# A product that needs no activations, moved to the head of a one-layer encoder step and carried through DRAM; the third FFN pair's splits moved ahead of the second pair's convolution

## The chip, the cores and the metric

The kernel runs on one core of one Trainium2 chip. The metric is the device time of one execution in microseconds: 2164.75 us before, the median of three runs (2163.62, 2164.75 and 2166.86). The profile is of one further execution, which took 2162.19 us.

## The reference, cut to what matters

One trunk layer over 1024 prompt frames and 64 sample frames (T = 1088 columns in the kernel), D_MODEL = 1024, D_FF = 2816, PLE_DIM = 256, all in fp32:

```
h = rms_norm(x, norm_mix)
glu_a, glu_b, q, k, v, gates = split(h @ w_in)
c = silu(layer_norm(dwconv31(glu_a * sigmoid(glu_b)))) @ w_conv_out
a = band_attention(q, k, v) @ w_att_out
x = x + (sigmoid(gate_c) * c + sigmoid(gate_a) * a) @ w_out
h = rms_norm(x, norm_ffn)
up, gate = split(h @ w_ffn_up)
x = x + (gelu(dwconv3(up)) * gate) @ w_ffn_down
h = rms_norm(x, norm_ple)
x = x + sigmoid(h @ w_ple_gate) * (p @ w_ple_proj)
y = rms_norm(x, norm_final)
```

`p` is an input, so `p @ w_ple_proj` (256 by 1024) depends on nothing that the layer computes.

## The kernel before

Everything lies feature-major: a tile holds 128 features (partitions) by T columns, and the columns go in three groups `GR` of 384, 384 and 320. An fp32 product is made of three passes over values split into a high and a low part (high by high, high by low, low by high): the lines L159 to L161 in the helper `mm3`, L817 to L819 in the head, L1171 to L1173 in the FFN. So a 1024-deep product for 128 output features and one group is 24 matmuls. Weights come raw from DRAM on SP's DMA queue (`w_load`); ACT makes the high part (L134, L797), DVE the low part (L135, L800). The program is written under a manual schedule: each engine runs its instructions in the order in which the code issues them, and waits only where an operand or a buffer is not ready.

**Head.** Fourteen warm-up matmuls (L743) keep TensorE busy while x arrives. The squares of the first group of x are taken by ACT (L754) and added by DVE (L761), TensorE sums them over the partitions (L770), POOL takes the power (L782), and TensorE spreads the result over the partitions (L216, `hr_ps`); twelve more warm-ups (`W2`) stand around that. Then a loop over slots `sl` follows, whose contents are set by tables (`SQ`, `ADD`, `COL`, `TOT`, `SPR`, `LAG`, `HDVE`): in a slot DVE makes one normalized tile `hn` (L187), ACT its high part `hT` (L189), DVE or POOL its low part (L181), and TensorE multiplies the tiles of earlier slots with the first two weight units (`gb` and `ga`). Behind the three groups, the ordinary jobs over the other units of `w_in` begin, `q` first.

**FFN.** The up projection works in pairs of units i = 0..21. Pairs 0 and 1 are plain. From pair 2 on a pair is computed as seven products of half size (A11·B11, S2·T2, A12·B21, S1·T1, S3·T3, S4·B22, A22·T4, in this order, 24 matmuls of 272 columns in each half, so 24 per product), whose operands are sums of activations (`comb`, T1 to T4) and of weights (`prep_a`, `prep_b`, `prep_c`; high parts by ACT L1148, sums by DVE L1157, low parts by DVE L1065). A result takes two of six PSUM banks, and is emptied by ACT (`put`, L1247) or by DVE into a sum (`add`, L1254). The convolution of a pair, `conv_a`, is one ACT pass (L1272), two DVE taps (L1275) and a gelu on ACT (L1277). Before the change, `conv_a(1)` stands ahead of pair 2, and `comb("T1")` and `prep_b(2)` behind pair 2's first `put`.

**Tail.** The down projection runs in four chunks of units. In the last one a generator `ple_prep` loads p and `w_ple_proj` (POOL's queue) and splits them. Then `ple(f, g)` makes for each feature tile f and group g the 24 matmuls with `w_ple_gate` and the 6 of p with `w_ple_proj` (L159 to L161, `pj<-pP,wpp`), a tanh on ACT (L1574), and two DVE operations (L1575, which reads the p product in PSUM, and L1578). The square and its sum for the final norm follow (L1017, L1018). Two further strands of work hang in a queue with due times and are forced where a stage needs them: `norm_ple` of the next group (hn L187, high part L189, low part L181 on POOL) and the split of the next weight unit (`wbig`, L134 and L135). The statistics of a group go through L202 (TensorE), L203, L206 (the power on POOL) and L216 (`sp_ps`).

In the changed kernel the line numbers are higher: by 1 in the helpers (L187 is L188, L135 is L136), by 66 in the head (L761 is L827), by 95 in the FFN (L1148 is L1243, L1254 is L1349), by 74 in the last stage (L1575 is L1649).

Of the kernel before, what the change touches and what calls it, by code (L numbers as in the profile page):

```python
# [16 lines left out]
P = 128  # L17
# [58 lines left out]
def encoder_step(ctx: ExitStack, tc: tile.TileContext, I, O):  # L76
# [143 lines left out]
    with tc.manual_schedule():  # L220
# [40 lines left out]
        for g, (c0, n) in enumerate(GR):  # L261
            for f in range(KT):
                dma_in(out=xt[f][:, c0:c0 + n], in_=I["x"][:, f, c0:c0 + n])
            if g == 0:
                w_load()
                dma_in(out=ident, in_=I["ident"])
                dma_in(out=par, in_=I["par"])
                w_load()
# [13 lines left out]
        hsq = [at.tile([P, KW], F32, tag=f"K{h}", name="hsq") for h in range(2)]  # L282
        hd = {}
# [512 lines left out]
        def w_hi(u, a, b):  # L796
            nc.scalar.activation(out=w2[u][:, 0, a:b, :], in_=raws[u][:, a:b, :], func=AF.Copy)  # L797
# [43 lines left out]
        for f in range(KT):  # L841
            head_acc(0, f)
            head_add(0, f)
        w_hi(0, 0, KT)
# [12 lines left out]
        ws["split"] = ws["used"] = 2  # L857
        for sl in range(3 * KT + 3 + LAG[2]):
            g, k = divmod(sl, KT)
            if g < 3:  # L860
                if k == 0:
                    begin(g)
                next(parts[g])
                pre(sl)
                if k == KT - 1:
                    next(parts[g])
            if 0 <= sl - 1 < 3 * KT:
                prod("gb", *divmod(sl - 1, KT))
# [483 lines left out]
        def prep_b(i):  # L1352
            wq[i, "A22"] = w_one()
            w_high(i, "A22")
            w_low(i, "A22")
            wq[i, "S1"], wq[i, "S3"] = w_two()
            w_high(i, "S1")
            w_sum(i, "S3")
            w_high(i, "S3")
            wq[i, "A12"] = w_one()  # L1360
            w_high(i, "A12")
            w_low(i, "S1")
            w_low(i, "S3")
            w_low(i, "A12")
# [84 lines left out]
        pP, wpp, h3, rows = [], [], [], []  # L1449

        def ple_prep():

            praw = bp.tile([P, 2, T], F32, tag="pb", name="praw")
            dma_st(out=praw, in_=I["p"])
            wraw = bp.tile([P, KT, 2, P], F32, tag="pb", name="wraw")
            dma_st(out=wraw, in_=I["w_ple_proj"])
            yield
            for k in range(2):
                t = bp.tile([P, 2, T], F32R, tag="pb", name="pP")
                split_into(t, 0, T, praw[:, k, :])  # L1460
                pP.append(t)
                yield
            wpp.extend(bp.tile([P, KT, 2, P], F32R, tag="pb", name="wpp") for _ in range(2))
            nc.scalar.activation(out=wpp[0], in_=wraw, func=AF.Copy)
            nc.vector.tensor_tensor(out=wpp[1], in0=wraw, in1=wpp[0].bitcast(F32), op=ALU.subtract)
            yield
# [16 lines left out]
        ple_it = ple_prep()  # L1483
        for ci, ch in enumerate(chunks[:-1]):
# [23 lines left out]
            for f in range(f0, KT):  # L1508
# [15 lines left out]
                if ci == 2:  # L1524
                    if f < 2:
                        next(ple_it)
                    if f in ROWS:
                        rows.append(w_use())
# [37 lines left out]
        def ple(f, g, hl):  # L1566
# [96 lines left out]
```

## Time and profile before

| | before |
|---|---|
| median of three runs | 2164.75 us |
| the profiled execution | 2162.19 us |
| its span, first to last instruction | 2160.1 us |
| TensorE (PE) busy | 2120.9 us, 98% of the span |
| VectorE (DVE) busy | 1361.8 us, 63% |
| ScalarE (ACT) busy | 829.3 us, 38% |
| GpSimd (POOL) busy | 229.1 us, 11% |
| mean granted TensorE clock | 0.995 of full speed |
| moved by DMA | 192.54 MB, 93 GB/s over the span |

The span is what the profile's times count from; the execution's own time is 2.1 us longer. Times in rows are microseconds from the start of the span. A row of a timeline gives the start, the duration (for several instructions that follow each other: from the first's start to the last's end), engine, line, operation, output and inputs, sizes and count, and in brackets how long the engine had been idle and what it waited for. A matmul's duration includes its way through the array: matmuls overlap, so what one costs is the distance of two starts.

### The profile page before, as it was taken

Reading aid. Unit: us, or ns where it says so; the run is one execution under the profiler, and the core shown is the slowest. Engines: PE = TensorE matmul, PEld = TensorE weight load, DVE = VectorE, ACT = ScalarE, POOL = GpSimd, SP = SyncE. Lnnn points to the kernel's source line nnn. Section 1 sums busy time; section 2 is a strip of 40 time slices with the busy share of each in tenths; the row PEclk is TensorE's granted clock in tenths of the full one; section 3 lists DMA queues with packets and bytes.
Section 4 is the critical chain, followed back from the end, with each engine's and each line's share of the span. In section 5 each row is a group of like instructions: output and inputs, shape, how many; then the busy total and the mean of one; then the engine's idle time right before and its main releaser. Section 6 shows DMA issues by size and latency. Waiting matters only on the chain.

```text
span 2160.1 us, 35720 instructions
## 1 busy us (share of the span) xinstructions
PE 2120.9 (98%) x14544; PEld 2088.8 (97%) x14544; DVE 1361.8 (63%) x2310; ACT 829.3 (38%) x1695; POOL 229.1 (11%) x455
## 2 busy tenths in 40 slices
PE   8999999999999999999999998999999999999997
PEld 6999999999999999999999998999999999999997
DVE  6877777777776756443254557777777763345644
ACT  5443535444444446562022334333333331113421
POOL 5110101101010101110000000000000020000400
PEclk9999999999999999999999999999999999999999
DMA  3312121212121222125433341122121253331011
GB/s 135 110 38 93 62 89 48 95 52 88 51 88 52 93 75 70 65 74 193 170 129 110 118 141 51 67 84 84 67 90 61 80 203 128 125 117 46 11 59 54
DMA packets 64708, 192.54 MB, mean 89 GB/s; under 512 B 8368, under 2 KB 22976, under 8 KB 63200
## 3 DMA queue, kind: packets, MB, share of 16 engines
q1 hardware_dynamic: 43072, 104.00, 14.2%
q0 software_dynamic: 21328, 85.71, 11.1%
q8 instruction: 114, 1.87, 0.3%
q10 hardware_dynamic: 144, 0.56, 0.1%
q14 instruction: 50, 0.41, 0.1%
HBM read 146.18 MB, written 54.01 MB: 93 GB/s over the span
## 4 chain that ended last, share of the span: by engine, by line
PE 84%; issue 7%; DVE 4%; ACT 2%; DMA 1%; POOL 1%; POOLq 0%; SPq 0%; DVEq 0%; ACTq 0%
PE pj L159 14%; PE pj L161 13%; PE pj L160 13%; PE pj L1173 7%; PE pj L1171 7%; PE pj L1172 7%; PE o_ps L520 5%; PE pj L1474 3%; PE pj L1473 3%; PE pj L1472 3%; PE t_ps L504 3%; PE s_ps L481 2%; PE s_ps L483 2%; DVE acc L1018 1%; DMA out_k_new<-kst 1%
## 5 line engine op out<-in xcount | busy, mean ns | idle before, releaser
L159 PE MATMUL pj<-hT,whl 128*128 128x384 f32 (+1 forms) x1296 | 442.0, 341 | 3.7 <-ACT kst L705 1.8
L161 PE MATMUL pj<-hT,whl 128*128 128x384 f32 (+1 forms) x1296 | 424.8, 328 | 0.3 <-DVE whl L135 0.3
L160 PE MATMUL pj<-hT,whl 128*128 128x384 f32 (+1 forms) x1296 | 424.1, 327 | 0.0
L327 DVE SCALAR_TENSOR_TENSOR c<-u,cc,c 128x1118 f32<-128x1118 f32 x240 | 331.0, 1379 | 3.2
L159 PEld LDWEIGHTS pj<-hT,whl 128*128 128x128 f32 x1296 | 244.1, 188 | 8.3 <-ACT kst L705 2.8
L161 PEld LDWEIGHTS pj<-hT,whl 128*128 128x128 f32 x1296 | 243.5, 188 | 0.6 <-DVE whl L135 0.6
L160 PEld LDWEIGHTS pj<-hT,whl 128*128 128x128 f32 x1296 | 244.1, 188 | 0.0
L1171 PE MATMUL pj<-mp,wq 128*128 128x272 f32 x704 | 203.9, 290 | 5.9 <-ACT wq L1148 5.9
L1173 PE MATMUL pj<-mp,wq 128*128 128x272 f32 x704 | 204.2, 290 | 0.0
L1172 PE MATMUL pj<-mp,wq 128*128 128x272 f32 x704 | 203.7, 289 | 0.0
L134 ACT ACTIVATE whl<-raw 128x1024 fp32r<-128x1024 f32 (+3 forms) x100 | 100.2, 1002 | 220.4 <-PE pj L1474 132.8
L135 DVE TENSOR_TENSOR whl<-raw,whl 128x1024 fp32r<-128x1024 f32 (+3 forms) x100 | 115.7, 1158 | 86.3 <-ACT whl L134 86.0
L1148 ACT ACTIVATE wq<-raw 128x512 fp32r<-128x512 f32 x144 | 84.4, 625 | 189.8 <-DVE raw L1157 124.0
L487 DVE CUSTOM_DVE_ANT_0 s<-s_ps,bias 128x640 f32<-128x640 f32 (+3 forms) x144 | 95.2, 661 | 90.3 <-PE s_ps L483 82.1
L1474 PE MATMUL pj<-gp,whl 128*128 128x384 f32 (+1 forms) x432 | 141.2, 327 | 0.6 <-DVE whl L135 0.6
L1473 PE MATMUL pj<-gp,whl 128*128 128x384 f32 (+1 forms) x432 | 141.2, 327 | 0.3 <-DVE gp L1382 0.3
L1472 PE MATMUL pj<-gp,whl 128*128 128x384 f32 (+1 forms) x432 | 141.0, 326 | 0.0
L1171 PEld LDWEIGHTS pj<-mp,wq 128*128 128x128 f32 x704 | 133.8, 190 | 6.1 <-ACT wq L1148 6.1
L520 PEld LDWEIGHTS o_ps<-v,pt 128*128 128x128 f32 (+2 forms) x1120 | 133.5, 183 | 6.4 <-issue 4.0
L1172 PE MATMUL pj<-bq,wq 128*128 128x272 f32 x480 | 138.4, 288 | 0.0
L1173 PE MATMUL pj<-bq,wq 128*128 128x272 f32 x480 | 138.2, 288 | 0.0
L1171 PE MATMUL pj<-bq,wq 128*128 128x272 f32 x480 | 138.0, 287 | 0.0
(260 smaller groups left out, 4901.3 us busy)
## 6 DMA issues: line engine op xcount, KB each, us to landing
raw<-in_w_in SPq DMA_DIRECT2D x56, 512.0 KB, 3.2
raw<-in_w_ffn_up SPq DMA_DIRECT2D x44, 512.0 KB, 4.4
q_d<-ug POOLq DMA_DIRECT2D x22, 544.0 KB, 3.0
gp<-q_d POOLq DMA_DIRECT2D x22, 544.0 KB, 7.1
tg<-s_d POOLq DMA_DIRECT2D x16, 544.0 KB, 3.9
aP<-a_d POOLq DMA_DIRECT2D x8, 1088.0 KB, 6.0
a_d<-aT POOLq DMA_DIRECT2D x64, 128.0 KB, 2.2
f_d<-e_d POOLq DMA_DIRECT2D x16, 383.5 KB, 4.9
```

The lines of the kernel that those rows point to most:

```text
L135: nc.vector.tensor_tensor(out=hl[:, 1, 0:k, :], in0=raw[:, 0:k, :], in1=hl[:, 0, 0:k, :].bitcast(F32), op=ALU.subtract)
L159: nc.tensor.matmul(ps, lhsT=wsel(hl, 0, k), rhs=r[:, 0, c0:c0 + n], start=(k == 0), stop=False)
L160: nc.tensor.matmul(ps, lhsT=wsel(hl, 0, k), rhs=r[:, 1, c0:c0 + n], start=False, stop=False)
L161: nc.tensor.matmul(ps, lhsT=wsel(hl, 1, k), rhs=r[:, 0, c0:c0 + n], start=False, stop=(k == K - 1))
L327: nc.vector.scalar_tensor_tensor(out=c_t[f], in0=u_t[f][:, j:j + CCOL], scalar=pc("conv_dw", f * CW + j), in1=c_t[f], op0=ALU.mult, op1=AL ...
L520: nc.tensor.matmul(o_ps[0:m, 0:64], lhsT=pt[0:w, b * P:b * P + m], rhs=c["v"][0:w, st["vb"] + b, h * 64:h * 64 + 64], start=(b == 0), stop ...
L1171: nc.tensor.matmul(ps, lhsT=q[:, 0, kt, :], rhs=h, start=start and kt == 0, stop=False)
L1172: nc.tensor.matmul(ps, lhsT=q[:, 0, kt, :], rhs=l, start=False, stop=False)
L1173: nc.tensor.matmul(ps, lhsT=q[:, 1, kt, :], rhs=h, start=False, stop=stop and kt == 3)
L1472: nc.tensor.matmul(ps, lhsT=hl[:, 0, k, :], rhs=h, start=k == 0, stop=False)
L1473: nc.tensor.matmul(ps, lhsT=hl[:, 0, k, :], rhs=l, start=False, stop=False)
L1474: nc.tensor.matmul(ps, lhsT=hl[:, 1, k, :], rhs=h, start=False, stop=k == K - 1)
```

## The change

1. **The product of p at the head.** p is loaded by groups and `w_ple_proj` by feature tiles, on SP's queue: 20 loads (`p_load`, `wp_load`), of which 6 of p and 2 of the weight stand ahead of the first group of x, 2 in the middle of it, 2 behind it; tiles 6 and 7 come behind all of x. ACT and DVE split them (`p_split` L320 and L322, `wp_split` L327 and L328). `p_proj(f)` makes 6 matmuls for each group (L339 to L341), 144 in all. A result is copied out of PSUM (L346 on ACT where 3f+g is even, L344 on DVE where it is odd) into the upper half of the raw p buffer, at the columns of its group: one staging place per group, so that the copy of tile f+1 waits until the store of tile f has read it. The store to DRAM (`p_d`, L347) goes by POOL's queue, 24 stores. Tiles 0 to 5 stand ahead of the first slot, tiles 6 and 7 in slots 1 to 6 (`PSL`). The squares of x's first group stand behind the passes 0, 1 and 2, as two, two and four; the statistics stand behind pass 3, the spread behind pass 4, the split of the first two weight units between. The twelve warm-ups `W2` go.
2. **FFN.** `comb("T1")` and `prep_b(2)` move ahead of `conv_a(1)`, and `prep_b` splits A12 first in every pair.
3. **Tail.** `ple_prep` goes, with its two loads and its splits. Eight loads of 544 KB bring `p_d` back into SBUF (`p2t`) at the start of the last chunk. `ple(f, g)` has no product of p any more; its first DVE operation reads `p2t`.

```diff
+PSL = {1: (6, 0, "t"), 2: (6, 1, "t"), 3: (6, 2, "s"), 4: (7, 0, "s"), 5: (7, 1, "t"), 6: (7, 2, "s")}
-W2 = (6, 6)
...
+        p_load(0)
+        wp_load(0)
+        wp_load(1)
+        p_load(1)
+        p_load(2)
+        x_load(0, range(0, 4))
+        wp_load(2)
+        wp_load(3)
+        x_load(0, range(4, 8))
+        dma_in(out=ident, in_=I["ident"])
+        wp_load(4)
+        wp_load(5)
+        w_load()
+        dma_in(out=par, in_=I["par"])
+        w_load()
+        x_load(1, range(KT))
+        x_load(2, range(KT))
...
+        def p_proj(f, gs=range(3), ps_of=None):
+            w = wpr[f % 4]
+            for g in gs:
+                c0, n = GR[g]
+                ps = ps_of if ps_of is not None else pjp.tile([P, 512], F32, tag="pj", name="pj")
+                for k in range(2):
+                    h, l = [x[:, c0:c0 + n] for x in ppt[k]]
+                    nc.tensor.matmul(ps[:, 0:n], lhsT=w[:, 0, k, :], rhs=h, start=k == 0, stop=False)
+                    nc.tensor.matmul(ps[:, 0:n], lhsT=w[:, 0, k, :], rhs=l, start=False, stop=False)
+                    nc.tensor.matmul(ps[:, 0:n], lhsT=w[:, 1, k, :], rhs=h, start=False, stop=k == 1)
+                sg = praw[1][:, c0:c0 + n]
+                if (3 * f + g) % 2:
+                    nc.vector.tensor_copy(sg, ps[:, 0:n])
+                else:
+                    nc.scalar.activation(out=sg, in_=ps[:, 0:n], func=AF.Copy)
+                dma_st(out=p_d[f][:, c0:c0 + n], in_=sg)
...
+        p_split(0)
+        wp_split(0)
+        p_split(1)
+        p_split(2)
+        wp_split(1)
+        p_proj(0)
...
+        acc0((0, 1))
+        p_proj(1)
+        wp_split(2)
+        acc0((2, 3))
+        p_proj(2)
+        wp_split(3)
+        acc0((4, 5, 6, 7))
+        p_proj(3)
         head_col(0, 0)
         head_tot(0, 0)
         head_col(0, 1)
         head_tot(0, 1)
+        wp_split(4)
+        p_proj(4)
+        w_hi(0, 0, KT)
+        head_spread(0)
         w_lo(0, 0, KT, nc.vector)
+        wp_split(5)
         w_hi(1, 0, KT)
         w_lo(1, 0, 4, nc.gpsimd)
         w_lo(1, 4, KT, nc.gpsimd)
-        warm(W2[0])
-        head_spread(0)
-        warm(W2[1])
+        p_proj(5)
...
         def prep_b(i):
+            wq[i, "A12"] = w_one()
+            w_high(i, "A12")
+            w_low(i, "A12")
             wq[i, "A22"] = w_one()
...
         plain(1, 2, 1)
+        comb("T1")
+        prep_b(2)
         conv_a(1)
         for i in range(2, NF):
             last = i == NF - 1
             put(i, "g0", both(banks(), i, "A11", "B11"))
             if i == 2:
-                comb("T1")
-                prep_b(2)
                 up_load(3, (0,))
...
+        for j in range(4):
+            t = bp.tile([P, 2, T], F32, tag="pb", name="p2t")
+            for k in range(2):
+                dma_st(out=t[:, k, :], in_=p_d[2 * j + k])
+            p2t.append(t)
...
-            p2 = pjt()
-            mmg(p2[:, 0:n], None, pP, c0, n, K=2, wsel=lambda _, s, k, f=f: wpp[s][:, f, k, :])
             z = tmp384()
             nc.scalar.activation(out=z[:, 0:n], in_=ps[:, 0:n], func=AF.Tanh, scale=0.5)
-            nc.vector.scalar_tensor_tensor(out=z[:, 0:n], in0=z[:, 0:n], scalar=1.0, in1=p2[:, 0:n], op0=ALU.add,
+            nc.vector.scalar_tensor_tensor(out=z[:, 0:n], in0=z[:, 0:n], scalar=1.0, in1=p2t[f // 2][:, f % 2, c0:c0 + n], op0=ALU.add,
                                            op1=ALU.mult)
```

DVE in the head, before: the sums of the squares, the statistics, the low part of the first weight unit, then the first normalized tiles.

```order
L761 TENSOR_TENSOR hsq<-hsq 128x384 x6
L777 TENSOR_SCALAR cc<-st_ps 128x3
L779 TENSOR_TENSOR cc<-cc,st_ps 128x3
L800 TENSOR_TENSOR whl<-raw,whl 128x1024
L187 SCALAR_TENSOR_TENSOR hn<-xt,cc,hr_ps 128x384 x3
L181 TENSOR_TENSOR hT<-hn,hT 128x384
L187 SCALAR_TENSOR_TENSOR hn<-xt,cc,hr_ps 128x384
```

DVE at the same place now (`wpr` is a split tile of `w_ple_proj`, `praw` the staging place, `pj` and `p_ps` the PSUM banks of the p product):

```order
L866 TENSOR_TENSOR whl<-raw,whl 128x1024
L328 TENSOR_TENSOR wpr<-wraw,wpr 128x256
L344 COPY praw<-pj 128x384
L344 COPY praw<-pj 128x320
L188 SCALAR_TENSOR_TENSOR hn<-xt,cc,hr_ps 128x384
L328 TENSOR_TENSOR wpr<-wraw,wpr 128x256
L188 SCALAR_TENSOR_TENSOR hn<-xt,cc,hr_ps 128x384 x2
L182 TENSOR_TENSOR hT<-hn,hT 128x384
L328 TENSOR_TENSOR wpr<-wraw,wpr 128x256
L344 COPY praw<-p_ps 128x384
L188 SCALAR_TENSOR_TENSOR hn<-xt,cc,hr_ps 128x384
```

Two copies of pass 5 stand in front of the first `hn`, and between the `hn` of the first group stand the splits of the tiles 6 and 7 and a copy of pass 6.

ACT at the second pair of the FFN, before: the convolution's two passes (L1272, L1277) stand ahead of T1 (`mp`) and of the weight splits.

```order
L1272 ACTIVATE ct<-ug,cc 128x1090
L1277 ACTIVATE ct<-ct 128x1090
L1247 ACTIVATE ug<-pj 128x272 x2
L1058 ACTIVATE mp<-x 128x544 x4
L1148 ACTIVATE wq_13030<-raw 128x512
L1148 ACTIVATE wq_13033<-raw 128x512 x2
```

ACT at the same place now:

```order
L1153 ACTIVATE mp<-x 128x544 x4
L1243 ACTIVATE wq_13247<-raw 128x512
L1243 ACTIVATE wq_13250<-raw 128x512
L1243 ACTIVATE wq_13253<-raw 128x512 x2
L1367 ACTIVATE ct<-ug,cc 128x1090
L1372 ACTIVATE ct<-ct 128x1090
L1342 ACTIVATE ug<-pj 128x272 x2
```

T1 and four weight splits stand ahead of both passes of the convolution, and the emptying of A11·B11 (L1342, `put`) behind them.

DVE in the tail, at the end of the first features' first two groups, before: `hn` of the last tile of the third group (128x320) stands ahead of the second feature's second group (L1575, 128x384).

```order
L135 TENSOR_TENSOR wbig<-raw,wbig 128x1024
L187 SCALAR_TENSOR_TENSOR tmp_19487<-x,cc,sp_ps 128x320
L1575 SCALAR_TENSOR_TENSOR tmp_19487<-tmp_19487,pj 128x384
L1578 SCALAR_TENSOR_TENSOR x<-tmp_19487,x 128x384
L1018 TENSOR_TENSOR acc_19486<-acc_19486,tmp_19487 128x384
L135 TENSOR_TENSOR wbig<-raw,wbig 128x1024
L1575 SCALAR_TENSOR_TENSOR tmp_19487<-tmp_19487,pj 128x320
```

DVE at the same place now:

```order
L188 SCALAR_TENSOR_TENSOR tmp_19732<-x,cc,sp_ps 128x320 x3
L1649 SCALAR_TENSOR_TENSOR tmp_19732<-tmp_19732,p2t 128x384
L1652 SCALAR_TENSOR_TENSOR x<-tmp_19732,x 128x384
L1113 TENSOR_TENSOR acc_19731<-acc_19731,tmp_19732 128x384
L136 TENSOR_TENSOR wbig<-raw,wbig 128x1024
L188 SCALAR_TENSOR_TENSOR tmp_19732<-x,cc,sp_ps 128x320
L1649 SCALAR_TENSOR_TENSOR tmp_19732<-tmp_19732,p2t 128x320
```

The last `hn` of the third group now stands behind that feature's three operations and behind a weight split, directly ahead of the third group's own first result.

## Rows read from the trace of the kernel before

**Rows 1.** The page: TensorE's share, and the chain of waits that ended last, by engine.

```profile
PE 2120.9 (98%) x14544; PEld 2088.8 (97%) x14544; DVE 1361.8 (63%) x2310; ACT 829.3 (38%) x1695; POOL 229.1 (11%) x455
...
PE 84%; issue 7%; DVE 4%; ACT 2%; DMA 1%; POOL 1%; POOLq 0%; SPq 0%; DVEq 0%; ACTq 0%
```

**Rows 2.** Busy time by stretch, head (columns: stretch, length, engines, clock, DMA share, GB/s).

```profile
7.14:17.18 10.04, 7.91 (x31) 5.00 (x31) 5.45 (x11) 6.18 (x12) 4.67 (x4) 0.66 1.04 373
17.18:28.35 11.17, 9.82 (x58) 8.40 (x56) 9.07 (x19) 5.23 (x13) 8.53 (x9) 1.00 0.44 160
28.35:51.30 22.95, 21.34 (x127) 19.03 (x126) 16.62 (x32) 12.28 (x28) 13.01 (x16) 1.00 0.01 1
```

**Rows 3.** Timeline of PE, head: the first product, the first job.

```profile
17.18 0.52 PE L817 MATMUL pj<-hT,whl 128*128 128x384 f32 x1
...
51.30 0.37 PE L159 MATMUL pj<-hT,whl 128*128 128x384 f32 x1
```

**Rows 4.** Timeline of DVE, head.

```profile
6.41 3.05 DVE L761 TENSOR_TENSOR hsq<-hsq 128x384 f32<-128x384 f32 x6 [5.20 <-ACT hsq L754]
...
15.43 1.66 DVE L187 SCALAR_TENSOR_TENSOR hn<-xt,cc,hr_ps 128x384 f32<-128x384 f32 x3 [2.56 <-PE hr_ps L216]
...
25.74 0.16 DVE L777 TENSOR_SCALAR cc<-st_ps 128x3 f32<-128x3 f32 x1 [1.19 <-PE st_ps L770]
...
27.15 0.60 DVE L187 SCALAR_TENSOR_TENSOR hn<-xt,cc,hr_ps 128x384 f32<-128x384 f32 x1
```

**Rows 5.** DMA issues: KB each, median us to landing.

```profile
s_d<-sg POOLq DMA_DIRECT2D x30, 192.0 KB, 2.2
...
xt<-in_x SPq DMA_DIRECT2D x16, 192.0 KB, 4.3
```

**Rows 6.** Groups by line and form, ACT: a copy of 384 columns out of PSUM.

```profile
L715 ACT ACTIVATE vst<-pj 128x384 f32<-128x384 f32 x16 | 7.9, 491 | 34.9 <-DMA out_k_new<-kst 23.0 <-PE pj L161 11.9
```

**Rows 7.** Timeline of PE, tail: blocks of six matmuls of p, and what follows each.

```profile
2039.66 0.33 PE L159 MATMUL pj<-pP,wpp 128*128 128x384 f32 x1
...
2040.70 0.33 PE L159 MATMUL pj<-gp,whl 128*128 128x384 f32 x1
...
2049.41 0.31 PE L159 MATMUL pj<-pP,wpp 128*128 128x320 f32 x1
...
2050.29 0.31 PE L159 MATMUL pj<-gp,whl 128*128 128x320 f32 x1
```

**Rows 8.** Timeline of PE, FFN pair 2: A12·B21, first of S1·T1, S4·B22.

```profile
1335.65 0.60 PE L1171 MATMUL pj<-mp,wq 128*128 128x272 f32 x1 [5.87 <-ACT wq L1148]
...
1341.38 0.29 PE L1173 MATMUL pj<-mp,wq 128*128 128x272 f32 x1
...
1347.51 0.29 PE L1171 MATMUL pj<-mp,wq 128*128 128x272 f32 x1
```

**Rows 9.** Busy time by stretch, FFN pair 2 (columns as in rows 2).

```profile
1335.00:1340.00 5.00, 4.35 (x17) 4.04 (x18) 4.15 (x9) 2.23 (x5) 0.77 (x3) 0.50 0.45 160
```

**Rows 10.** Timeline of ACT, FFN pair 2.

```profile
1324.10 1.29 ACT L1272 ACTIVATE ct<-ug,cc 128x1090 f32<-128x1090 f32 x1
1328.20 1.12 ACT L1277 ACTIVATE ct<-ct 128x1090 f32<-128x1090 f32 x1 [2.81 <-DVE ct L1275]
...
1329.77 2.29 ACT L1058 ACTIVATE mp<-x 128x544 fp32r<-128x544 f32 x4
```

**Rows 11.** Timeline of DVE, tail: last `hn` of the third group, and what stood behind it.

```profile
2046.42 0.54 DVE L187 SCALAR_TENSOR_TENSOR tmp<-x,cc,sp_ps 128x320 f32<-128x320 f32 x1
2047.88 0.55 DVE L1575 SCALAR_TENSOR_TENSOR tmp<-tmp,pj 128x384 f32<-128x384 f32 x1 [0.91 <-ACT tmp L1574]
...
2050.63 1.22 DVE L135 TENSOR_TENSOR wbig<-raw,wbig 128x1024 fp32r<-128x1024 f32 x1 [0.39 <-ACT wbig L134]
```

**Rows 12.** Timeline of POOL, tail: the power, and the last low part of the third group.

```profile
2031.88 1.16 POOL L206 TENSOR_TENSOR cc<-cc 128x3 f32<-128x3 f32 x1
...
2047.54 0.88 POOL L181 TENSOR_TENSOR h<-tmp,h 128x320 fp32r<-128x320 f32 x1 [4.29 <-ACT h L189]
```

More of the change, by code (lines that the diff above doesn't have):

```diff
@@ L260, in encoder_step @@
         xt = [xc.tile([P, CCOL], F32, tag="xc", name="xt") for _ in range(KT)]
[L261 to L268, printed above, removed]
+        p_d = dram.tile([KT, P, T], F32, name="p_d")
         nc.vector.memset(ones, 1.0 / D)
@@ L282, in encoder_step @@
         hsq = [at.tile([P, KW], F32, tag=f"K{h}", name="hsq") for h in range(2)]
+        praw = [xc.tile([P, UW], F32, tag="u", name="praw", bufs=2) for _ in range(2)]
+        ppt = [[at.tile([P, UW if tg == "lnb" else T], F32R, tag=tg, name="pp") for tg in tgs]
+               for tgs in (("Q0", "Q1"), ("vst", "lnb"))]
+        wraw = at.tile([P, 6, 2, P], F32, tag="v", name="wraw")
+        wpr = [at.tile([P, 2, 2, P], F32R, tag="pt", name="wpr", bufs=2) for _ in range(2)]
+        wpr += [at.tile([P, 2, 2, P], F32R, tag=f"bias{h}", name="wpr") for h in range(2)]
@@ new lines, in p_load, with wp_load, x_load @@
+        def p_load(g):
+            c0, n = GR[g]
+            for k in range(2):
+                dma_in(out=praw[k][:, c0:c0 + n], in_=I["p"][:, k, c0:c0 + n])
+        def wp_load(f):
+            dma_in(out=wraw[:, f % 6], in_=I["w_ple_proj"][:, f])
+        def x_load(g, fs):
+            c0, n = GR[g]
+            for f in fs:
+                dma_in(out=xt[f][:, c0:c0 + n], in_=I["x"][:, f, c0:c0 + n])
+        p_load(0)
[3 more added lines that the diff above has]
+        p_load(2)
@@ new lines, in encoder_step, with p_split @@
+        x_load(0, range(0, 4))
[10 more added lines that the diff above has]
+        x_load(2, range(KT))
+        def p_split(g):
+            c0, n = GR[g]
+            for k in range(2):
+                nc.scalar.activation(out=ppt[k][0][:, c0:c0 + n], in_=praw[k][:, c0:c0 + n], func=AF.Copy)
+            for k in range(2):
+                nc.vector.tensor_tensor(out=ppt[k][1][:, c0:c0 + n], in0=praw[k][:, c0:c0 + n],
+                                        in1=ppt[k][0][:, c0:c0 + n].bitcast(F32), op=ALU.subtract)
@@ L840, in encoder_step, with acc0 @@
         warm(WARM)
[L841 to L844, printed above, removed]
+        p_split(0)
[4 more added lines that the diff above has]
+        p_proj(0)
+        def acc0(fs):
+            for f in fs:
+                head_acc(0, f)
+                head_add(0, f)
+        acc0((0, 1))
[6 more added lines that the diff above has]
+        p_proj(3)
         head_col(0, 0)
@@ L872, in encoder_step @@
             post(sl)
+            if sl in (0, 2):
+                wp_split(6 + sl // 2)
+            if sl in PSL:
+                f, g, x = PSL[sl]
+                if x not in p_ps:
+                    p_ps[x] = (ps_t if x == "t" else ps_s).tile([P, 2, 512], F32, tag=x, name="p_ps")
+                    p_ps[x + "n"] = 0
+                p_proj(f, (g,), p_ps[x][:, p_ps[x + "n"] % 2, :])
+                p_ps[x + "n"] += 1
             for x in range(3):
@@ L1448, in encoder_step @@
             dma_st(out=xr[f], in_=x_d[f])
[L1449 to L1466, printed above, removed]
+        h3, rows, p2t = [], [], []
         def down(ps, hl, gs, g, ks, K):
@@ L1523, in encoder_step @@
                     g_split(nxt[0][0])
[L1524 to L1528, printed above, removed]
+                if ci == 2 and f in ROWS:
+                    rows.append(w_use())
         new_acc(384)
@@ L1534, in encoder_step @@
         h3.extend(gs)
+        h3.extend([bp.tile([P, 2, T], F32R, tag="pb", name="h3") for _ in range(KT - nk)])
+        for j in range(4):
+            t = bp.tile([P, 2, T], F32, tag="pb", name="p2t")
+            for k in range(2):
+                dma_st(out=t[:, k, :], in_=p_d[2 * j + k])
+            p2t.append(t)
         for g, (c0, n) in enumerate(GR):
```

17 lines of the change are left out of this document (9 added, 8 removed).

## The prediction

> **What bounds the kernel now.** The page's shares come first: TensorE is busy for 98% of the span and makes 84% of the chain that ended last [rows 1]. So a matmul that goes is worth its cadence, work for other engines is free where TensorE keeps running, and the change decides itself in the few places where it does not. The table by stretch shows the largest: between 7.14 us and the first job at 51.30, TensorE works at two thirds of its clock until the first product at 17.18, and is then busy 9.82 of 11.17 and 21.34 of 22.95 us [rows 2, 3]; warm-up matmuls are in the first figure. Next I read the head's timeline of DVE, since what starts a product there is the normalized tile `hn`: its first starts at 15.43 behind the squares' sums, its last of the first group at 27.15 [rows 4]. The third view is TensorE's timeline at FFN pair 2, with a wait of 5.87 us [rows 8], and the fourth the tail, where the six matmuls per tile and group that go can be seen between the others [rows 7].
>
> **Tail: what is removed.** A block of six took 2040.70 − 2039.66 = 1.04 us with 384 columns and 2050.29 − 2049.41 = 0.88 with 320 [rows 7]. There are 16 of the one and 8 of the other: 16.6 + 7.0 = −23.6 us. Not all of it stays. The units of feature 0 and 1 run while the norms of the next groups are made by DVE, ACT and POOL at their own pace, and the removed blocks were cover for that. Before, the last `hn` of the third group starts at 2046.42, and its low part on POOL ends 2.0 us later, at 2048.42 [rows 11, 12], ahead of its use. Now the order puts this `hn` behind feature 1's middle group: behind its two DVE operations, the sum of the square and a weight split. From the first of these to the split's end passed 2050.63 + 1.22 − 2047.88 = 4.0 us [rows 11]; with some 0.8 for the tanh ahead and the 2.0 behind, the low part is ready 6.8 us behind the middle group's last product, and TensorE wants it after 21 products and one, 22 × 0.146 = 3.2: a pause of 3.6. By the same working the low parts of the second group come 1.4 us late in feature 0, and the spread, which loses the block between it and the statistics, waits 1.15 for the power of 1.16 [rows 12]. About 0.9 us of pauses that stood there before fall into these. 1.4 + 1.15 + 3.6 − 0.9 = +5.2, and the last tanh, which ran beside the last block, adds 0.4. **Tail: −23.6 + 5.6 = −18.0.** The eight loads of `p2t` lie beside the last chunk's some 50 us of products and cost nothing; without that cover, their 4.5 MB at 373 GB/s [rows 2] would cost 12.
>
> **Head, up to the first norm.** What is added: 144 matmuls at the cadences 1.04/6 = 0.174 and 0.88/6 = 0.146 [rows 7], a pass of three groups 12 × 0.174 + 6 × 0.146 = 2.96 us; 8 passes 23.7. But a pass can't follow another at that pace, for a group has one staging place: a copy out of PSUM (0.49 [rows 6]), the store until it lands, then the next copy. No row shows a store from this place beside the head's loads. The nearest below is a store of the same size on the same queue in a quiet stretch, 2.2 us; the nearest above, the head's own loads of that size in full traffic, 4.3 [rows 5]. I take 3.2, between them, since the queue is the former's and the traffic the latter's. A turn is 0.49 + 3.2 + 0.1 = 3.8. The passes 0 to 2 end at 10.2, 13.5 and 17.5 (the first right behind p's splits and the warm-ups' end at 7.14). ACT and DVE run in order, so the last four squares stand behind the copies of pass 2, which wait for the stores of pass 1: squares at 18.7 to 20.7, sums at 21.2, against 9.46 before (6.41 + 3.05 [rows 4]). Pass 3 ends at 22.6; statistics 24.0; pass 4 27.0; spread 28.0; pass 5 waits for its weight split, which stands behind that of the first `w_in` unit, and runs from 29.0 to 32.65. DVE's two copies of pass 5 stand in front of `hn`: first `hn` at 33.2 against 15.43, **+17.8**. With 2.2 us for the landing it would be 1 us less, with 4.3 2.3 more.
>
> The Trainium skill (DMA: Bandwidth & Descriptors, § SWDGE vs HWDGE vs iDMA) says that DMAs of GpSimd and of SP feed different queues inside each DMA engine, which takes turns between them. By it a store would not wait behind the loads that are queued, and its landing would lie near the quiet row; the sum would come out some 1 us lower.
>
> **Head, the first group's slots.** From the first to the last `hn` before: 27.15 − 15.43 = 11.7 us. DVE gets in between: two splits of `w_ple_proj` and copies of passes 6 and 7. Own work 0.37 × 2 + 0.5 × 3 = 2.2; waits for ACT, which makes the high parts behind queued squares, 1.5 and 2.3; waits for the copies' matmuls, which TensorE reaches only behind the products of that slot, 2.0 and 2.2. Less about 1 us of the wait for the statistics that stood there (1.19 [rows 4]): **+9.1**. An idle 0.6 ahead of the next group's `hn` goes. Beyond, TensorE is full [rows 2] and nothing changes. **Head: +26.3**, the first job at 77.6 instead of 51.30. POOL issues 24 stores more, some of them ahead of the power and of the low parts; it is idle for more than half of that time [rows 2]. The tiles 6 and 7 of the weight land near 33 us by 373 GB/s [rows 2], 2 us before they are used.
>
> **FFN.** Before, A12·B21 waits 5.87 us for its split and then runs at half clock: 1335.65 to 1341.4, 5.75 us for 24 matmuls which take 3.0 at the cadence 0.125, at a granted clock of 0.50 in that stretch [rows 8, 9]. The lost time is 5.87 + 2.75 = 8.6 and S4·B22 starts at 1347.51. Now ACT makes T1 (2.29) where the convolution began, at 1324.10 [rows 10], A12 is split by 1327, and A12·B21 follows S2·T2 without a wait, 1329.6 to 1332.6. But ACT's two convolution passes and the gelu's wait for DVE (1.29, 2.81, 1.12 [rows 10]) now stand ahead of the copies that empty A11·B11's banks, at 1335.0. With six banks, two each for A11·B11, S2·T2 and A12·B21, S1·T1 has none and waits 2.9 us; S3·T3 waits 0.45 for the sum that empties S2·T2's banks, S4·B22 3.5 for the next sum, which stands on DVE behind T4 and more splits. S4·B22 starts at 1345.4: **−2.1**. The pause moves more than it goes. In later pairs A12 first costs nothing, since splits there are done a product ahead.
>
> **Sum.** 26.3 − 2.1 − 18.0 = +6.2: the profiled execution goes from 2162.19 to 2168.4, and the median, which stands 2.56 above it, to **2171.0**. A measurement of this kernel can tell about 0.2%, 4.3 us, from no change.
>
> **Rivals.**
> *A, faster: the copies in the head never hold ACT or DVE.* Then TensorE's time sets the head: it has at most the 10.04 us ahead of the first product and the 1.35 + 1.61 of gaps behind it [rows 2] to spare, 13.0 for the 23.7 of p, so the head grows by 10.7: 10.7 − 2.1 − 18.0 = −9.4, 2155.4. It comes out faster by over 4.3 us where the head grows by less than 2.1 + 18.0 − 4.3 = 15.8, so that, with 9.1 − 0.6 for the slots, the first `hn` starts before about 22.7. For it: the stores may land at 2.2 us. Against: ACT's and DVE's fixed order, in which the squares stand behind copies. 0.15.
> *B, no change: the third group's norm is not late.* The tail then keeps 23.6 − 0.4 = 23.2, and the sum is +1.0: 2165.8. For it: POOL and ACT are nearly idle in the tail; against: `hn` stands behind a split in the order. 0.22.
> *C, slower: the clock falls in the new pauses.* In the head, TensorE has gaps from pass 1 on, and the warm-ups that filled such gaps are gone; before, it had 0.66 of its clock in 10 us with twelve of them [rows 2]. At half clock a pass takes 5.9 instead of 2.96 and no longer hides beside the staging turn of 3.8: 2.1 more for each of three to five passes; in the FFN the price is 2.75 a product [rows 8]. 2173.8 with the FFN's alone, 2180 with three passes of the head's. The Trainium skill (TensorE: Matmul & The Clock Gate, § Why this matters for your kernels) asks for no gaps between products for this reason. 0.10.
> *The forecast* has the rest, 0.53; by the ends of the store's landing (−1.0, +2.3) and the errors of the waits, 0.04 of it falls within 0.2%.
>
> **How the numbers follow.** Faster 0.15 (A). Same 0.22 + 0.04 = 0.26. Slower 0.49 + 0.10 = 0.59. The range leaves out most of A and the far end of C: it runs from **2159 to 2182**. The likeliest case's own range is 2167 to 2176.
>
> **What would show it.** First `hn` of the head near 33, its last of the first group near 54, first job near 77.6. DVE's and ACT's waits in the head named after the landing of `p_d`. In the FFN three pauses of about 2.9, 0.45 and 3.5 us, released by ACT's `put` and DVE's `add`, and none ahead of A12·B21. In the tail a pause of about 3.6 us ahead of the last of feature 0's third-group products, released by POOL's low part. Wrong would be: a first `hn` before 22.7 (A), no pause in the tail (B), a granted clock near 0.5 in the head's passes or behind the FFN's pause (C).

## The result and the profile after

The changed kernel takes 2198.19 us (median of 4 runs, 2195.3 to 2200.5) against 2165.01 (median of 4, 2163.62 to 2166.86): slower by a factor of 1.0157, 95% interval 1.0144 to 1.017. The forecast was 2171.0 with a range to 2182; the side was right, and the time lies 16 us above the range. The profiled execution's span is 2194.3 us against 2160.1, +34.2.

Where the 34.2 us lie is read by marks, instructions that both kernels have, at their start in both TensorE timelines:

| mark on TensorE | before | after | later by | forecast |
|---|---|---|---|---|
| first job of the unit `q` | 51.30 | 90.91 | 39.6 | 26.3 |
| A11·B11 of pair 2 | 1323.61 | 1361.00 | 37.4 | 26.3 |
| S4·B22 of pair 2 | 1347.51 | 1383.04 | 35.5 | 24.2 |
| last chunk's second matmul | 1968.87 | 2013.71 | 44.8 | 24.2 |
| first matmul of the third group, feature 0 | 2045.90 | 2088.50 | 42.6 | |
| the same, feature 1 | 2050.29 | 2100.71 | 50.4 | |
| end of the span | 2160.1 | 2194.3 | 34.2 | 6.2 |

The page of the changed kernel, TensorE's share and the chain by engine, answers to [rows 1]:

```profile
PE 2132.5 (97%) x14532; PEld 2098.6 (96%) x14532; DVE 1370.1 (62%) x2333; ACT 835.7 (38%) x1718; POOL 245.6 (11%) x485
...
PE 81%; issue 8%; DVE 4%; DMA 3%; ACT 2%; POOL 1%; SPq 0%; POOLq 0%; DVEq 0%; ACTq 0%
```

DMA has gone from 1% to 3% of the chain, from some 22 us to some 66.

**Head.** Busy time by stretch in the changed kernel (columns as in [rows 2]):

```profile
6.36:14.29 7.93, 5.69 (x33) 5.03 (x31) 3.28 (x7) 3.70 (x9) 1.81 (x3) 1.00 1.04 348
14.29:28.75 14.46, 10.41 (x42) 8.77 (x43) 5.25 (x11) 5.30 (x13) 4.32 (x8) 0.76 1.01 378
28.75:44.89 16.14, 13.57 (x56) 12.46 (x54) 4.33 (x9) 4.57 (x9) 6.88 (x9) 0.68 0.45 145
44.89:67.00 22.11, 16.76 (x92) 15.84 (x93) 10.53 (x24) 8.07 (x19) 11.82 (x15) 0.92 0.20 75
```

TensorE is not full, DVE and ACT are less than half busy, and the granted clock (the third figure from the right) is 0.76 and 0.68 between 14.29 and 44.89, from the end of pass 1 to pass 5. What the copies wait for stands in DVE's timeline:

```profile
13.67 0.56 DVE L344 COPY praw<-pj 128x384 f32<-128x384 f32 x1 [4.23 <-DMA p_d<-praw]
...
21.34 0.56 DVE L344 COPY praw<-pj 128x384 f32<-128x384 f32 x1 [2.84 <-DMA p_d<-praw]
...
35.37 0.56 DVE L344 COPY praw<-pj 128x384 f32<-128x384 f32 x1 [3.66 <-PE pj L341]
...
44.89 0.61 DVE L188 SCALAR_TENSOR_TENSOR hn<-xt,cc,hr_ps 128x384 f32<-128x384 f32 x1
...
67.41 1.65 DVE L188 SCALAR_TENSOR_TENSOR hn<-xt,cc,hr_ps 128x384 f32<-128x384 f32 x3
```

The copies wait for stores at first, for TensorE later. The first `hn` stands at 44.89, against 15.43 in [rows 4]; the eighth, the first of the three at 67.41, against 27.15. What the instructions on the buffer `praw` waited for up to 40 us (us, times), and, from the view of the tile `p_d` in the same stretch, the time from a store's issue to its landing:

```profile
  DMA p_d<-praw: 18.9, 6
  PE pj L341: 17.5, 6
```

```profile
DMA to landing us min/median/max: 2.1/4.8/6.0
```

The two ends belong to different traffic. Of the stores issued up to 28.75 us, while the queues moved 348 and 378 GB/s, the landing is 4.1/4.9/6.0; of those from 28.75 to 45, at 145 GB/s, it is 2.1/2.7/4.1.

TensorE's timeline shows the low clock inside a pass, and the wait of pass 5 for its weight split:

```profile
18.10 0.52 PE L339 MATMUL pj<-pp,wpr 128*128 128x384 f32 x1
18.42 0.52 PE L340 MATMUL pj<-pp,wpr 128*128 128x384 f32 x1
...
38.61 0.45 PE L339 MATMUL pj<-pp,wpr 128*128 128x384 f32 x1 [1.11 <-ACT wpr L327]
```

The distance of two starts is 0.32 us here, where [rows 7] has 0.174.

**FFN pair 2**, TensorE's timeline, the three pauses in place of the one in [rows 8]:

```profile
1372.87 0.40 PE L1266 MATMUL pj<-mp,wq 128*128 128x272 f32 x1 [2.67 <-ACT ug L1342]
1376.38 0.39 PE L1266 MATMUL pj<-bq,wq 128*128 128x272 f32 x1 [0.25 <-DVE ug L1349]
1383.04 0.37 PE L1266 MATMUL pj<-mp,wq 128*128 128x272 f32 x1 [3.39 <-DVE ug L1349]
```

**Third chunk of the down projection.** Here is a wait that the kernel before does not have. TensorE's timeline, then POOL's, then the chain of waits (start, us, what):

```profile
1965.65 0.69 PE L1550 MATMUL pj<-gp,whl 128*128 128x384 f32 x1 [5.43 <-ACT whl L135]
1967.02 0.69 PE L1552 MATMUL pj<-gp,whl 128*128 128x384 f32 x1 [0.36 <-DVE whl L136]
```

```profile
1944.38 2.08 POOL L1471 DMA_DIRECT2D gp<-q_d  x4 [70.75 <-PE pj L1552]
1946.45 2.60 POOL L1613 DMA_DIRECT2D p2t<-p_d  x5
1949.87 0.53 POOL L1613 DMA_DIRECT2D p2t<-p_d  x1 [0.81 <-DMA gp<-q_d]
```

```profile
1949.76 14.07 DMA raw<-in_w_ffn_down
1963.91 1.06 ACT wbig L135
```

The loads of `p2t` stand in the code behind the third chunk, whose last matmul is at 2013. POOL issues six of them at 1946 to 1950, right behind the four loads of the next chunk's units, and two weight loads issued from 1949.76 on, of 512 and 320 KB, take 14.1 us each. ACT splits the first (`wbig`, for the next chunk) and right behind it the second (`whl`, 1964.87), for which TensorE waits.

**Tail**, third group of feature 0. TensorE's timeline, then DVE's:

```profile
2091.96 0.42 PE L160 MATMUL pj<-h,whl 128*128 128x320 f32 x1 [1.55 <-ACT h L190]
2092.90 0.42 PE L161 MATMUL pj<-h,whl 128*128 128x320 f32 x1 [0.52 <-POOL h L182]
...
2099.07 0.64 PE L160 MATMUL pj<-h,whl 128*128 128x320 f32 x1 [3.30 <-ACT h L190]
```

```profile
2089.72 1.23 DVE L136 TENSOR_TENSOR wbig<-raw,wbig 128x1024 fp32r<-128x1024 f32 x1 [0.39 <-ACT wbig L135]
2090.87 1.46 DVE L188 SCALAR_TENSOR_TENSOR tmp<-x,cc,sp_ps 128x320 f32<-128x320 f32 x3
...
2096.83 1.22 DVE L136 TENSOR_TENSOR wbig<-raw,wbig 128x1024 fp32r<-128x1024 f32 x1 [0.39 <-ACT wbig L135]
2097.98 0.54 DVE L188 SCALAR_TENSOR_TENSOR tmp<-x,cc,sp_ps 128x320 f32<-128x320 f32 x1
```

Not one but four tiles of the third group are late, the tiles 4 to 6 behind one weight split, tile 7 behind the next. In [rows 11] the last was made at 2046.42, in time.

### The profile page after: what moved, and what is told of

The parts are those of the page before. It is cut to its first block, busy times and chain, and to the rows that moved or that the text cites. A ratio compares the mean times of both kernels' runs of the same rounds, so it can differ in the third digit from the quotient of the medians.

```text
span 2194.3 us, 35830 instructions
## 1 busy us (share of the span) xinstructions
PE 2132.5 (97%) x14532; PEld 2098.6 (96%) x14532; DVE 1370.1 (62%) x2333; ACT 835.7 (38%) x1718; POOL 245.6 (11%) x485
## 4 chain that ended last, share of the span: by engine, by line
PE 81%; issue 8%; DVE 4%; DMA 3%; ACT 2%; POOL 1%; SPq 0%; POOLq 0%; DVEq 0%; ACTq 0%
PE pj L160 13%; PE pj L162 13%; PE pj L161 13%; PE pj L1267 7%; PE pj L1268 7%; PE pj L1266 7%; PE o_ps L586 5%; PE pj L1552 3%; PE pj L1551 3%; PE pj L1550 3%; PE t_ps L570 3%; PE s_ps L549 2%; PE s_ps L547 2%; DMA p_d<-praw 1%; DMA raw<-in_w_ffn_down 1%
```

## The experiments

My theory behind the result: four separate losses. (1) In the head a copy waits for the store before it, and the order of splits makes TensorE wait, so passes run with gaps and then at the lower clock. (2) In the slots the copies of passes 6 and 7 hold up the norm. (3) The late loads run ahead on POOL's queue into a weight load. (4) The due times of the tail's norm count matmuls, and a unit has fewer now. The rivals: the clock alone sets the head, since the warm-ups are gone; and the losses behind the head only come with it.

The experiments ran in three groups (e1 to e4, e5 to e8, e9 to e11), each with runs of the kernel before, medians 2163.7, 2162.61 and 2163.9. Differences are taken to the one of the same group; the changed kernel stands at +33.2 against its own, 2165.01.

One caution for the head: it is the same code in the changed kernel, in e4_p2t_sp and in e5_due, and their profiled executions have the first `hn` at 44.89, 43.17 and 44.07. So a difference of under 2 us there shows nothing.

### The FFN part alone (e1_ffn)

Edit of the kernel before, part 2 of the change:

```diff
+        comb("T1")
+        prep_b(2)
         conv_a(1)
```

> The kernel before with the FFN part alone. Theory (the pause in front of A12*B21 is replaced by pauses behind the convolution, as the changed kernel's trace has it: 2.67, 0.25 and 3.39 us instead of 5.87 and a product at half clock): 1.9 us less than before, 2163.1 by the median of 2165.0. Rival (the part is neutral, or costs in later pairs, where A12's split now stands ahead of A22's): 2165 or more.

Measured: 2163.29 us, ratio 1.0000 (0.9991 to 1.001): what the part is worth can't be told from nothing. Its trace has the pauses 2.66, 0.25 and 3.36 us, and from A11·B11 to S4·B22 pass 1347.20 − 1325.18 = 22.0 us, 1.9 less than the 23.9 before, as expected. But behind the last pause the clock falls, which it did not do in the changed kernel. Busy time by stretch, this kernel and the changed one, each behind that pause:

```profile
1347.00:1352.00 5.00, 4.80 (x21) 4.83 (x22) 4.97 (x13) 1.02 (x3) 0.00 (x0) 0.50 0.00 0
1383.00:1388.00 5.00, 4.96 (x40) 5.00 (x41) 4.88 (x12) 1.00 (x2) 0.00 (x0) 1.00 0.00 0
```

S4·B22 takes 5.6 us here instead of 3.0, so in this execution the part loses more than the 1.9 that it gained. This is rival C's price in the FFN. Why the clock fell behind a pause of 3.36 here and not behind one of 3.39 there, no run shows.

### The tail part alone (e2_tail)

```diff
+            for k in range(2):
+                dma_st(out=t[:, k, :], in_=x_d[2 * j + k])
...
-            p2 = pjt()
-            mmg(p2[:, 0:n], None, pP, c0, n, K=2, wsel=lambda _, s, k, f=f: wpp[s][:, f, k, :])
```

> The kernel before with the tail part alone: no product of p anywhere; the eight late loads read the stored x instead of a product of p, so the kernel leaves p @ w_ple_proj out and multiplies by x. Theory (the loads run ahead on POOL's queue into the middle of the third chunk of the down projection and hold up a weight load there, 8.6 us; and the tail keeps only 10.6 of the 23.6 us of its removed products): 2.0 us less than before, 2163.0, with a wait of some 5 us released by the split of a down weight. Rival (both losses come only with the late head): 23 us less, 2142.

Measured: 2161.51, ratio 0.9987 (0.9978 to 0.9996), 2.2 us less. TensorE's timeline has both waits, without any change in the head:

```profile
1931.14 0.69 PE L1455 MATMUL pj<-gp,whl 128*128 128x384 f32 x1 [5.21 <-ACT whl L134]
...
2064.15 0.63 PE L159 MATMUL pj<-h,whl 128*128 128x320 f32 x1 [3.63 <-ACT h L189]
```

The rival falls: losses 3 and 4 belong to the tail part itself, and eat nearly all of the 23.6 us.

### Two staging places (e3_stage2)

```diff
-                sg = praw[1][:, c0:c0 + n]
+                sg = praw[f % 2][:, c0:c0 + n]
```

> The changed kernel with two staging places per group (odd tiles in one half of the raw p buffer, even tiles in the other), so that a copy waits for the store of the tile before the last. Theory 1 (the staging turn sets the head's pace, and the low clock follows from its gaps): first hn near 34 instead of 44.9, 9 to 11 us less, 2188. Theory 2 (the clock, since the warm-ups are gone, and the order of squares and copies set it): first hn stays above 42, at most 3 us less.

Measured: 2189.4, +25.7 against before, 7.5 less than the change. DVE's timeline:

```profile
11.57 0.56 DVE L344 COPY praw<-pj 128x384 f32<-128x384 f32 x1 [1.64 <-PE pj L341]
...
37.25 0.60 DVE L188 SCALAR_TENSOR_TENSOR hn<-xt,cc,hr_ps 128x384 f32<-128x384 f32 x1
```

The copy that waited 4.23 us for a store at 13.67 now comes at 11.57 and waits for its matmuls. First `hn` 37.25 instead of 44.89 (43.17 and 44.07 in the other two): between the two theories' numbers, nearer to the first. So the one staging place costs 6 to 7.6 us. Part of that was in the forecast, which had a turn of 3.8; and with the second place, where a copy waited for a store only once, for 1.2 us, the first `hn` is still 4 us behind the forecast of 33.2. Something else holds these: most of passes 4 and 5 still runs at 0.32 us a matmul, behind the statistics and behind a split.

### The late loads on SP's queue (e4_p2t_sp)

```diff
-                dma_st(out=t[:, k, :], in_=p_d[2 * j + k])
+                dma_in(out=t[:, k, :], in_=p_d[2 * j + k])
```

> The changed kernel with the eight late loads on SP's queue, where they stand behind the weight loads, instead of POOL's. Theory (on POOL's queue they run some 55 us early and slow a weight load of the third chunk from 4 to 14 us): the wait of 5.43 us and the slow clock behind it go, 8.4 us less, 2189.8, and the weight's landing is back near 4 us. Rival (the weight load is slow for another reason, such as its own small packets beside the gelu products' loads): no change, 2198.

Measured: 2188.2, +24.5, 8.7 less than the change. The weight loads between 1900 and 2010 us, in the change and in this kernel, minimum, median and maximum to landing:

```profile
DMA to landing us min/median/max: 2.8/3.1/14.1
```

```profile
DMA to landing us min/median/max: 2.8/3.4/4.8
```

The wait is gone from TensorE's list. Loss 3 is shown, in place and size. What is not parted is the queue from the time: on SP's queue the loads stand behind the weight loads and start some 60 us later, so the run does not say whether loads on SP's queue at the early time would have done the same. That the four loads of the units alone do no harm, the kernel before shows: no weight load from 1865 to 1980 us takes over 5.1 us there. SP's timeline:

```profile
2006.71 4.11 SPq L1613 DMA_DIRECT2D p2t<-p_d  x8
```

### Earlier due times in the tail (e5_due)

```diff
-            norm_to(g, "norm_ple", h3, 3600 if g < 1 else 4500, 1800, 1500 if g < 2 else 1200)
+            norm_to(g, "norm_ple", h3, 3600, 1400, 1200 if g < 2 else 600)
```

> The changed kernel with earlier due times for the three norms of the tail (steps of 1200 instead of 1500, and 600 instead of 1200 for the third group). Theory (the due times count matmuls; a unit of the last stage now has 24 instead of 30, so fewer steps are issued in each, and the third group's last five tiles fall behind a weight split and two results): its waits of 1.55, 0.52, 0.42, 3.30 and 0.30 us and the slow clock behind them go, 8 to 10 us less, 2189. Rival (DVE and ACT can't make the tiles earlier): the waits appear one unit earlier, at most 3 us less.

Measured: 2189.21, +26.6, 6.6 less than the change. TensorE's waits from 1900 us on, by releaser (us in total, times, longest):

```profile
PE st_ps L203 <- DVE acc L1113: 8.3, 3, 2.9
PE pj L1550 <- ACT whl L135: 5.2, 1, 5.2
PE sp_ps L217 <- POOL cc L207: 1.3, 1, 1.3
```

No tile of a norm is waited for any more. A part came back: in the change the waits of `st_ps` were 3.9 in two, here 8.3 in three, since the statistics are issued before the sums of squares are done. So it is more than the rival allowed and less than I expected; where that extra 4.4 goes is seen, how to avoid it was not tried.

### Warm-up matmuls between the passes (e6_warm)

```diff
             for g in gs:
+                if ps_of is None and f:
+                    warm(3)
```

> The changed kernel with three warm-up matmuls ahead of each group of the passes 1 to 5. Theory 1 (the staging turn makes gaps, the gaps the half clock in passes 2, 4 and 5, and that about 6 us of the head): granted clock over 0.95 from 14 to 45 us, first hn at 39 to 41 instead of 44.9, 3 to 6 us less, 2193. Theory 2 (TensorE's pace does not matter in the head, since each copy waits for a store anyway): first hn at 44 to 46, no change.

Measured: 2199.4, +36.8, not faster. Busy time by stretch:

```profile
14.29:28.75 14.46, 12.33 (x63) 8.17 (x62) 5.81 (x12) 4.90 (x13) 3.77 (x7) 1.00 1.03 384
28.75:44.89 16.14, 12.89 (x75) 9.60 (x73) 4.85 (x10) 6.07 (x13) 8.13 (x12) 1.00 0.53 182
```

The clock is at its full level throughout, as theory 1 said, but the first `hn` stands at 43.42, no earlier than in e4_p2t_sp, which has the head without these warm-ups (43.17). The run does not tell the theories apart as cleanly as I meant it to: the warm-ups that keep the clock also take TensorE's time. What it does show: a clock kept up with matmuls of no use gained nothing here, and at full clock the copies of the passes 1 and 2 on DVE, at 14.89 and 22.58, still wait 4.88 and 4.08 us for a store.

### All repairs (e7_all), and with warm-ups (e8_all_warm)

Two staging places, SP's queue, due times, and splits ahead of copies:

```diff
         acc0((2, 3))
+        wp_split(3)
         p_proj(2)
-        wp_split(3)
         acc0((4, 5, 6, 7))
+        wp_split(4)
         p_proj(3)
...
-        wp_split(4)
+        wp_split(5)
         p_proj(4)
```

> The changed kernel with two staging places, the late loads on SP's queue, the earlier due times, and the weight splits of tiles 3 to 5 ahead of the copies they stood behind. If the causes are separate, the gains add: 8.8 (two places) + 10.0 (SP's queue) + 9 (due times) + 2 (splits) = 30, 2168; if the due times do nothing, 2177.

> The same with two warm-up matmuls ahead of each group of the passes 1 to 5. If the half clock of the passes 4 and 5 still costs 4 us behind the other repairs: 2164, the kernel before within 0.2%. If TensorE's own time already sets the head, the warm-ups add theirs: 2170.

Measured: 2174.08 (ratio 1.005, 1.0035 to 1.0066) and 2173.52 (1.0049, 1.0034 to 1.0064). The three gains of e3 to e5 add to 22.8; the sum of all is 33.2 − 11.5 = 21.7. They are separate. What the splits add to the whole can't be told, since the four runs of e7_all lie between 2170.78 and 2176.37; they moved the first `hn` from 37.25 to 31.31, but the eighth only from 59.80 to 57.24. Busy time by stretch up to the first `hn` of e7_all:

```profile
14.29:31.31 17.02, 14.59 (x88) 13.49 (x88) 8.37 (x18) 8.41 (x18) 8.64 (x13) 1.00 1.04 394
```

The granted clock is 1.00 with no warm-up added. So the rival that the clock alone sets the head, since the warm-ups are gone, falls: once most waits for stores and splits were gone, the clock stayed up by itself. With it falls the premise of e8_all_warm, that the passes 4 and 5 still run at half clock. There the warm-ups cost time, as its second theory had it: the first `hn` stands at 35.27 and the first job at 84.13, against 80.71 in e7_all. DVE's timeline of e7_all:

```profile
31.31 0.60 DVE L188 SCALAR_TENSOR_TENSOR hn<-xt,cc,hr_ps 128x384 f32<-128x384 f32 x1
...
56.83 0.49 DVE L344 COPY praw<-p_ps 128x320 f32<-128x320 f32 x1 [4.63 <-PE p_ps L341]
57.24 1.66 DVE L188 SCALAR_TENSOR_TENSOR hn<-xt,cc,hr_ps 128x384 f32<-128x384 f32 x3
```

From the first to the eighth `hn` now pass 25.9 us, against 22.5 in the change and 11.7 before, the last 4.6 of it for a copy of pass 7 that stands in front of `hn` and waits for TensorE. Both kernels stay slower than the one before, and by the medians the warm-ups make no difference.

### Passes 6 and 7 behind the slots (e9_late2), and pass 5 too (e10_late3)

```diff
-            if sl in PSL:
-                f, g, x = PSL[sl]
...
+        for f in (6, 7):
+            p_proj(f)
         head_small()
```

> The kernel of e7_all with passes 6 and 7 behind the head's last slot instead of inside slots 1 to 6. Theory (in the slots their copies and splits hold DVE and ACT, which make the normalized tiles, and wait there for matmuls behind the slot's products): from the first to the eighth hn 12 to 13 us instead of 25.9, the two passes behind cost their TensorE time and a turn, 6 to 7 us: 6 us less, 2168. Rival (the slots are slow because of the squares of the next groups, which also run late): the stretch stays over 20 us and the passes come on top, 2180.

> The same with pass 5 behind the slots too. If a pass ahead of the first hn costs more than its TensorE time (its copies stand in front of hn on DVE, its matmuls wait for a split or run at half clock): first hn 3 to 5 us earlier than 31.3, the whole 0 to 2 us less than e9_late2. If TensorE's time alone counts: the same as e9_late2.

Both edits also give the late passes one staging place, and move the splits of the tiles 6 and 7 to slots 16 and 20.

Measured: 2172.69 (1.0043, 1.0027 to 1.006) and 2172.3 (1.0041, 1.0027 to 1.0055). DVE's timeline of e9_late2, first and eighth `hn`:

```profile
31.42 1.66 DVE L188 SCALAR_TENSOR_TENSOR hn<-xt,cc,hr_ps 128x384 f32<-128x384 f32 x3
...
44.45 0.60 DVE L188 SCALAR_TENSOR_TENSOR hn<-xt,cc,hr_ps 128x384 f32<-128x384 f32 x1
```

13.0 us, as the theory of loss 2 said; the rival falls. But the gain is 1.4 us by the medians, not 6, within what the runs scatter. From the eighth `hn` to the first job pass 34.2 us instead of 23.5 in e7_all: the two passes behind take 78.66 − 70.91 = 7.75, and the other 3 us the later groups' slots, for which I have no cause that a run has shown. In e10_late3 the first `hn` is later (32.48), against the expectation, and the granted clock is 0.80 and 0.76 in the stretches where e9_late2 has 1.00 and 0.89; the first job stands at 82.97 against 78.66, yet the medians are the same.

### What the tail can bring at most (e11_tail_good)

```diff
-                dma_st(out=t[:, k, :], in_=x_d[2 * j + k])
+                dma_in(out=t[:, k, :], in_=x_d[2 * j + k])
...
+            norm_to(g, "norm_ple", h3, 3600, 1400, 1200 if g < 2 else 600)
```

> The kernel of e2_tail (no head part, no product of p, multiplies by the stored x, which leaves p @ w_ple_proj out) with the late loads on SP's queue and the earlier due times: what the tail part can bring at most. Theory: 23.6 less the pauses of the first two groups and the last tanh, 20 us less than before, 2143.

Measured: 2144.97, ratio 0.9914 (0.9899 to 0.9929), 18.9 less than before. So the tail could give 19 us to a head that costs less than that. The best head tried (e9_late2, first job at 78.66) costs 27.4, more than the 23.7 us of its own matmuls. No version with the product at the head beats the kernel before.

## Why the prediction was wrong

**Right**: the side, and the plan of the sum. The head loses more than the tail gives. The 23.6 us of removed blocks are real: from feature 1's third-group unit to the end the change gains 50.4 − 34.2 = 16.2 us, which are 12 × 1.04 + 7 × 0.88 = 18.6 of blocks less 2.0 of clock (below) and 0.4 for the last tanh. FFN: −2.1 forecast, 35.5 − 37.4 = −1.9 in the trace, with pauses 2.67, 0.25 and 3.39 where 2.9, 0.45 and 3.5 stood. Slots: +9.1 forecast, 67.41 − 44.89 − 11.7 = +10.8 measured, though the wait for the statistics, which was to shrink by about 1, rose from 1.19 to 2.00. The pauses of the tail's first two groups: 1.4 + 1.15 − 0.9 = 1.65 forecast; measured 44.9 (the first unit, 2067.45 against 2022.57) to 42.6 is 2.3 gained of four blocks' 4.2, so 1.9.

**Wrong, head up to the first norm** (+17.8 forecast, +29.5 measured). The step that failed is the staging turn of 3.8 us. It took the landing of a store at 3.2, between 2.2 and 4.3 [rows 5]; while x was loading it was 4.9 in the median and up to 6.0, above the upper bound that I had kept. By the forecast's own rate, 2.3 us for 1.1 of landing, that is an estimate of 3.6 of the 11.7 by which the first `hn` missed 33.2. And it took the turn alone as the price, with TensorE at full pace beside it. The turns of the first group's copies were 5.3, 6.8, 5.7, 7.3 and 8.1 us (starts at 8.33, 13.67, 20.48, 26.20, 33.45, 41.52): the first two set by stores, the third by sums of squares that stand ahead on DVE, the last two by TensorE, which had by then fallen to the lower clock, with the statistics and a late split in between. e3_stage2 puts 6 to 7.6 us on the staging place, and the splits of e7_all take another 5.9; together this is more than the 11.7, since part of both was in the forecast. The rows part the 5.9: in e3_stage2 the slow matmuls of the passes 4 and 5 took 6.9 us, which take 3.7 at the cadences of [rows 7], so the clock has some 3.2; the waits for splits were 0.88 + 1.16 + 0.67 = 2.7. In e7_all both are gone. That the low clock follows from the gaps is what rival C had for the head, at 0.10; I kept it apart from the forecast, though the gaps were in the forecast itself.

The Trainium skill (DMA: Bandwidth & Descriptors, § SWDGE vs HWDGE vs iDMA) says that the engines take turns between the queues of GpSimd and SP. From that I worked out a landing near the quiet row, 2.2 us. The trace shows 4.9 in the median beside x's loads, as long as x's own loads of that size in the changed kernel (4.8): the measurement decides, and a queue of its own did not spare the store the traffic.

**Wrong, the eight loads of `p2t` "lie beside the last chunk's some 50 us of products and cost nothing"** (0 forecast; +8.7 measured, 44.8 against 36.1 at a late mark in the up projection, 1750.38 before and 1786.46 after). The price I named if the cover were gone was 12. What failed is the place: I took the loads to start where they stand in the code. Nothing on POOL held them there: POOL had waited for the gelu products' buffers, issued those loads, and went straight on. They met two weight loads. e4_p2t_sp shows that starting them later takes the loss away.

**Wrong, the tail's third group** (−18.0 forecast for the tail, 34.2 − 44.8 = −10.6 measured). The step: "a pause of 3.6" for the last tile. The unit came 50.4 − 42.6 + 0.88 = 8.7 us late by four tiles and not by one, and the next unit ran at the lower clock for 17 matmuls, 0.267 instead of 0.146, another 2.0. I had the order of DVE in front of me and read one row of it; the three tiles at its top come late too, behind the weight split at 2089.72. e5_due shows the cause: the steps are issued by due times that count matmuls, and each unit now counts 24 and not 30; with earlier due times no tile is waited for.

**Not foreseen, small**: between the first job and pair 2 the change gains 2.2 us, 2.0 of it in waits for `vst` and a gate copy (5.5 before, 3.5 after in the lists of TensorE's waits). No run was made on it.

Head (11.7 + 1.7, rounded), loads and tail are 13.3 + 8.7 + 7.4 us, less the 2.2; with 0.8 in the up projection (0.2 in pair 2, 0.6 in later pairs, which no run explains) the sum was wrong by 28 in the profile. All three erred to the same side: each took work that is off TensorE as covered.

Two slips in the prediction moved nothing. Rival B's +1.0 leaves out the 1.65 of pauses of the tail's first two groups, which do not hang on the third; with them it is +2.7, still no change. And POOL was not "idle for more than half of that time": by [rows 2] it was busy 26.2 of 44.2 us. It hardly held up a store all the same: ahead of 13 of the 15 stores up to 40 us POOL was idle.

## What to carry to other kernels

Work that is moved to fill an engine's idle time brings its own path with it: here splits, 24 copies and 24 stores. The first passes went at the pace of one buffer's turn and not of their matmuls; and the best head tried still cost 27.4 us for matmuls of 23.7, so that nothing of them was hidden. Before a transfer is called hidden, find what holds its issue back on its own queue: where it stands in the code is no start time, and what it meets there may be on the critical path. And where later work is released by a count of the work that you remove, the removal moves it.

## What the runs showed of the hardware that I had not expected

A 192 KB store from GpSimd's queue landed in 2.2 us in quiet; stores of 160 and 192 KB took 4.9 (median; 4.1 to 6.0) while the queues moved 348 to 378 GB/s, and 6.0 (4.5 to 7.4) in the same stretch with two staging places, where the copies do not wait for the stores. A 512 KB weight load that otherwise lands in 3 to 4 us took 14.1 beside ten loads of 544 KB from another queue. Warm-up matmuls brought the granted clock from 0.76 and 0.68 to 1.00 without making the program faster, and with the waits gone it was 1.00 without them. And behind pauses of nearly the same length, 3.36 and 3.39 us, the clock fell to 0.50 in one execution and stayed at 1.00 in another.
